# A fused two-layer trunk on one core: when the attention's queries and keys are prepared, and how close its steps stand together

## The chip, the core and the metric

The kernel is one program for one core of a Trainium2 chip. The core has a matrix engine (PE in the profile, with its weight loads shown apart as PEld), a vector engine (DVE), a scalar engine (ACT), a small general engine (POOL) and a queue that issues transfers (SP). Each works through its own list of instructions in a fixed order, and waits on semaphores for the others. The metric is the device time of one execution in microseconds (us), as the median of several runs.

## What is computed

A trunk of two layers over 512 positions of width 1024, all in float32. Layer 0 is forgetting attention with 16 heads of width 64, layer 1 a gated linear recurrence; each is followed by a gated feed-forward block with a causal convolution of width 3, and a last norm ends it. The change touches only the attention, which is in short:

```
proj = h @ w_in;  q, k, v, fl = split(proj)
c = cumsum(log_sigmoid(fl + b_f))                     # one running bias per head
logits = q @ k.T * scale + (c[t] - c[s])              # masked to s <= t
p = softmax(logits);  o = p @ v;  return o @ w_out
```

## The kernel before

**Precision and layout.** Activations are kept with the width on the 128 partitions and the 512 positions along the free axis. Each float32 matrix product is made of three products of a rounded high part and a low part (`mm3`, lines 85 to 87), so one 128x128 block of weights costs three matmuls over 512 columns. `chunk` loads a 512 KB block of weights into a `raw` tile (line 72) and `split` makes the high part on ACT (line 67) and the low part on DVE (line 68).

**Attention goes by pairs of heads.** Heads 2hp and 2hp+1 share 128 rows, so there are eight pairs. For a pair, `projections` makes three tiles of PSUM (values, queries, keys: `pj_v`, `pj_q`, `pj_k`, 24 matmuls each) and puts them in `queue`. It is the main stream of PE, and it runs up to three tiles ahead.

`operands` takes a tile from the queue. `values` scales and transposes it (`vT`) and splits it into `vh`, `vl`. `qk` scales it, splits it (ACT cast `qh` or `kh`, DVE subtraction `ql` or `kl`) and sends the pieces by small transfers into the four operand tiles `KX`, `QX`, `KK`, `QQ` of each head (lines 347 to 356). There are two sets of these tiles, so pair n writes over those of pair n-2.

`maxima` computes the row maxima of a pair: eight matmuls `mxp` (line 422) with `KX` and `QX`, each reduced on DVE (line 424, with a short read of the accumulator), in three PSUM banks named "s". The maxima go through a small transpose `rp` into `rrow` and by transfer into two more rows of `QX`.

`attend` does the softmax and the product with the values. `logits` makes one PSUM bank (`lg_a`, `lg_a`, `lg_c`, `lg_b`, `lg_b`, two banks in turn), takes the exponential on ACT into `pt` (line 464, two buffers), masks the diagonal blocks on POOL (line 466), casts on ACT to `ph` and subtracts on DVE to `pl`. `weigh` multiplies `ph` and `pl` with `vh`, `vl` into a bank `pv` (lines 480 to 482), `evacuate` copies it out on ACT (`dn`, `o`), and a reciprocal by logarithm and exponential on ACT (`rc`) with three DVE steps and a split gives `oh`, `ol`.

**What sets the order.** `conduct` (line 137) runs these generators together. Each turn takes one step of the main stream, which is one block of three matmuls, and then every side stream that is due. `yield 3` means due three turns later, `yield lambda: ...` means due as soon as the condition holds. Counters in `done` tie the streams together: `logits` counts pairs whose five logit tiles have been asked for, `out` counts pairs that are finished. A scheduler behind the language then lists the instructions of each engine, keeping near to the order in which they were asked for, but letting a later instruction pass an earlier one that it takes to be not ready. After the eighth pair the output projection `wo` takes over as the main stream (`early`), then the feed-forward block and the second layer, which the change does not touch.

Of the kernel before, what the change touches and what calls it, by code (L numbers as in the profile page):

```python
# [35 lines left out]
def trunk(ctx, tc, xT, gains, convs, bf, wqkv, wqkv0, wf, wo, wup, wdn, wh, wi, who, out):  # L36
# [12 lines left out]
    def side(name):  # L49

        return ps.tile([P, S], F32, tag="s", name=name)

    def lbank(name):
        return ps.tile([P, S], F32, tag="lg", name=name, bufs=2)
# [11 lines left out]
    def split(dst_h, dst_l, src):  # L66
        A.copy(dst_h, src)  # L67
        V.tensor_tensor(dst_l, src, dst_h.bitcast(F32), op=ALU.subtract)  # L68
# [161 lines left out]
    with tc.tile_pool(name="att", bufs=2, side="right") as ap_:  # L230
        def tmp(name, rows=P):
            return ap_.tile([rows, S], F32, tag="tmp", name=name, bufs=3)
# [13 lines left out]
        for i, (wa, wb, xa, xb) in enumerate(((0, 1, 0, 1), (1, 3, 1, 2), (3, 6, 2, 4), (6, 8, 4, 6), (8, 8, 6, 8))):  # L246
# [3 lines left out]
            if wb > wa:  # L250
                w = opool.tile([P, 4, 2, P], F32, name=f"wst{wa}", bufs=1, tag=f"ol{i}")
# [64 lines left out]
        def forget():  # L316

            z, e = tmp("fz", HEADS), tmp("fe", HEADS)
            A.copy(e, of[32:32 + HEADS])
            V.tensor_tensor(z, of[:HEADS], e, op=ALU.add)  # L320
            V.tensor_mul(z, z, rstd[:HEADS])
            V.tensor_scalar(z, z, bft, None, op0=ALU.add)
            V.scalar_tensor_tensor(e, z, -1.0, z, op0=ALU.mult, op1=ALU.max)
            A.activation(e, e, AF.Exp, scale=-1.0)
            A.activation(e, e, AF.Ln, bias=1.0)
            V.scalar_tensor_tensor(z, z, 0.0, e, op0=ALU.min, op1=ALU.subtract)
            m8 = tmp("m8", HEADS)
            G.memset(m8, 1.0)
            V.tensor_tensor_scan(e, m8, z, initial=0.0, op0=ALU.mult, op1=ALU.add)
            V.tensor_scalar(ch, e, -8.0, None, op0=ALU.mult)  # L330
            V.scalar_tensor_tensor(cl, e, -8.0, ch.bitcast(F32), op0=ALU.mult, op1=ALU.subtract)


        done = {"k": 0, "v": 0, "max": 0, "logits": 0, "out": 0}

        def qk(w, hp, o):
            nm = "qk"[w]
            t32 = tmp(f"{nm}32_{hp}")
            V.tensor_mul(t32, o, rstd)
            th = ap_.tile([P, S], F32R, tag="pth", name=f"{nm}h_{hp}", bufs=1)  # L340
            tl = ap_.tile([P, S], F32R, tag="ptl", name=f"{nm}l_{hp}", bufs=1)
            split(th, tl, t32)
            th, tl = th.bitcast(F32), tl.bitcast(F32)
            for e in range(2):
                r = slice(64 * e, 64 * e + 64)
                t = {n: a.bitcast(F32) for n, a in st[2 * (hp % 2) + e].items()}
                if w == 0:
                    nc.sync.dma_start(t["QX"][0:64], th[r])
                    nc.sync.dma_start(t["QQ"][0:64], tl[r])
                    nc.sync.dma_start(t["QQ"][64:128], th[r])  # L350
                else:
                    h = 2 * hp + e
                    nc.sync.dma_start(t["KX"][64:66], cc[h:h + 33:32].bitcast(F32))
                    nc.sync.dma_start(t["KX"][0:64], th[r])
                    nc.sync.dma_start(t["KK"][0:64], th[r])
                    nc.sync.dma_start(t["KK"][64:128], tl[r])
            done["k"] += w
# [18 lines left out]
        queue = []  # L376
# [16 lines left out]
        def operands():  # L393

            forget()
            qk(0, 0, oq)
            qk(1, 0, ok)
            values(0, ov)
            for hp in range(8):
                for w, n in ((2, hp), (0, hp + 1), (1, hp + 1)):  # L400
                    if n == 8 or (hp == 0 and w == 2):
                        continue
                    yield lambda: queue and done["out"] >= n - 1
                    w_, n_, o = queue.pop(0)
                    if w == 2:
                        values(n, o)
                    else:
                        qk(w, n, o)
# [33 lines left out]
        def attend():  # L442

            for hp in range(8):
                yield lambda: done["max"] > hp and done["v"] > hp
                yield 5
                tt = [st[2 * (hp % 2)], st[2 * (hp % 2) + 1]]
                vh, vl = vst[hp % 2]
                parts = {}

                def logits(key, *blocks):

                    nm = f"{hp}_{key}"
                    lg = lbank(f"lg_{nm}")
                    w = 0
                    for e, j, c in blocks:
                        n = S - P * j
                        reg = lg[:, c:c + n]
                        js = slice(j * P, (j + 1) * P)
                        t = tt[e]  # L460
                        PE.matmul(reg, t["KK"][:, js], t["QQ"][:, j * P:], start=True, stop=False)
                        PE.matmul(reg, t["KX"][0:68, js], t["QX"][0:68, j * P:], start=False, stop=True)
                    pt = ap_.tile([P, S], F32, tag="pt", name=f"pt_{nm}", bufs=2)
                    A.activation(pt, lg, AF.Exp, scale=0.125)
                    for e, j, c in blocks:
                        G.affine_select(out=pt[:, c:c + P], in_=pt[:, c:c + P], pattern=[[1, P]],
                                        compare_op=ALU.is_ge, fill=0.0, base=0, channel_multiplier=-1)
                    ph = ap_.tile([P, S], F32R, tag="ph", name=f"ph_{nm}", bufs=3)
                    pl = ap_.tile([P, S], F32R, tag="pl", name=f"pl_{nm}", bufs=3)
                    split(ph, pl, pt)  # L470
                    for e, j, c in blocks:
                        parts[e, j] = ph, pl, c

                def weigh(o, e, js):
                    cs = slice(64 * e, 64 * e + P)
                    for j in js:
                        ph, pl, c = parts[e, j]
                        s_ = slice(c, c + S - P * j)
                        oo = o[:, j * P:]
                        PE.matmul(oo, vh[:, j, cs], ph[:, s_], start=j == 0, stop=False)  # L480
                        PE.matmul(oo, vl[:, j, cs], ph[:, s_], start=False, stop=False)
                        PE.matmul(oo, vh[:, j, cs], pl[:, s_], start=False, stop=j == 2)

                dn = ap_.tile([P, S], F32, tag="dn", name=f"dn_{hp}", bufs=1)
                o32 = ap_.tile([P, S], F32, tag="o32", name=f"o32_{hp}", bufs=1)

                def evacuate(o, e):
                    a, b = slice(64 * e, 64 * e + 64), slice(64 - 64 * e, 128 - 64 * e)
                    A.copy(dn[a], o[b])
                    A.copy(o32[a], o[a])  # L490

                logits("a0", (0, 0, 0))
                yield 3
                logits("a1", (0, 1, 0), (0, 3, 384))
                yield 3
                logits("c", (0, 2, 0), (1, 2, 256))
                yield 3
                oa = side(f"pv_{hp}_0")
                weigh(oa, 0, (0,))
                logits("b0", (1, 0, 0))  # L500
                yield 2
                weigh(oa, 0, (1, 3))
                logits("b1", (1, 1, 0), (1, 3, 384))
                done["logits"] += 1
                yield 3
                weigh(oa, 0, (2,))
                evacuate(oa, 0)
                ob = side(f"pv_{hp}_1")
                weigh(ob, 1, (0,))
                yield 2  # L510
                weigh(ob, 1, (1, 3, 2))
                evacuate(ob, 1)
                rc = tmp(f"rc_{hp}")
                A.activation(rc, dn, AF.Ln)
                A.activation(rc, rc, AF.Exp, scale=-1.0)
                V.tensor_mul(dn, dn, rc)
                V.scalar_tensor_tensor(rc, dn, 2.0, rc, op0=ALU.subtract, op1=ALU.mult, reverse0=True)
                V.tensor_mul(o32, o32, rc)
                if hp % 2 == 0:
                    pair[:] = [opool.tile([P, 2, S], F32R, tag=f"{n}{hp // 2}", name=f"{n}{hp}", bufs=1)  # L520
                               for n in ("oh", "ol")]
                oh[hp], ol[hp] = (t[:, hp % 2] for t in pair)
                split(oh[hp], ol[hp], o32)
                done["out"] += 1
# [62 lines left out]
    with tc.tile_pool(name="hg", bufs=2, side="right") as hp_:  # L587
# [46 lines left out]
        done = {"core": 0, "out": 0}  # L634
# [270 lines left out]
```

## Time and profile before

| | |
|---|---|
| median of 3 runs | 1275.78 us (1275.57 to 1275.93) |
| the profiled execution, its own time | 1276.34 us |
| its span, from first to last instruction | 1274.6 us |
| PE busy | 1254.7 us, 98% of the span |
| DVE, ACT, POOL busy | 803.9, 590.8, 45.7 us |
| chain that ended last, share of PE | 93% |
| the attention's pairs, by the trace | about 50 to 240 us after the start |

A matmul that is issued right behind another starts about 0.23 us after it when it has 512 columns, though the profile shows it as 0.39 us long: matmuls overlap in the array. So time lost on PE is best read from the distance between starts. The idle time in brackets behind a row is shorter than that.

### The profile page before, as it was taken

The numbers are of one execution on the slowest core, as the hardware profiler recorded it, in microseconds if no ns is written. First come the engines' busy times: TensorE is split into PE (matmuls) and PEld (weight loads), VectorE is DVE, ScalarE is ACT, GpSimd is POOL, SyncE is SP. The second block draws the span as 40 slices with busy tenths as digits, with TensorE's granted clock in tenths as the row PEclk, the third lists the DMA queues.
The fourth block names the chain that finished last, engine by engine and source line by source line (L and its number), as shares of the span: only waits on it lengthen the run. The fifth ranks groups of instructions, "written<-read, shape, count | busy, mean of one in ns | idle before, by whom it ended". The sixth has DMA issues, their size and how long they took to land.

```text
span 1274.6 us, 15662 instructions
## 1 busy us (share of the span) xinstructions
PE 1254.7 (98%) x6002; PEld 1041.3 (82%) x6002; DVE 803.9 (63%) x1230; ACT 590.8 (46%) x830; POOL 45.7 (4%) x121
## 2 busy tenths in 40 slices
PE   8999999999999999999999999999999999999996
PEld 6777888888888888888888988987888888888886
DVE  6687667387777777333367585566777777762233
ACT  6366556464444444222266565554544444442231
POOL 2011110000000000000010000000000000000001
PEclk9999999999999999999999999999999999999999
DMA  5643454243333233333322222223233333323321
GB/s 179 170 135 98 130 130 132 83 133 99 100 100 99 93 93 93 91 96 102 95 84 83 81 69 83 84 67 91 91 100 99 100 98 91 94 89 94 97 83 66
DMA packets 42586, 127.25 MB, mean 100 GB/s; under 512 B 5536, under 2 KB 7840, under 8 KB 42512
## 3 DMA queue, kind: packets, MB, share of 16 engines
q1 hardware_dynamic: 41728, 125.52, 33.1%
q8 instruction: 47, 0.77, 0.3%
q10 hardware_dynamic: 688, 0.56, 0.1%
q0 software_dynamic: 96, 0.18, 0.1%
q14 instruction: 27, 0.22, 0.1%
HBM read 111.43 MB, written 2.10 MB: 89 GB/s over the span
## 4 chain that ended last, share of the span: by engine, by line
PE 93%; DVE 2%; ACT 2%; DMA 1%; issue 1%; POOL 0%; SPq 0%; DVEq 0%; ACTq 0%
PE pj_up L87 13%; PE pj_up L85 13%; PE pj_up L86 13%; PE pj_dn L85 6%; PE pj_dn L87 6%; PE pj_dn L86 6%; PE i L651 1%; PE i L650 1%; PE i L648 1%; PE pj_who L86 1%; PE pj_wo L85 1%; PE pj_wo L86 1%; PE pj_who L87 1%; PE pj_who L85 1%; PE pj_wo L87 1%; PE pj_hf L85 1%
## 5 line engine op out<-in xcount | busy, mean ns | idle before, releaser
L85 PE MATMUL pj_up<-xh_f,wh_up 128*128 128x512 f32 x704 | 273.9, 389 | 0.0
L86 PE MATMUL pj_up<-xl_f,wh_up 128*128 128x512 f32 x704 | 273.9, 389 | 0.0
L87 PE MATMUL pj_up<-xh_f,wl_up 128*128 128x512 f32 x704 | 273.9, 389 | 0.0
L86 PEld LDWEIGHTS pj_up<-xl_f,wh_up 128*128 128x128 f32 x704 | 132.1, 188 | 27.6
L87 PEld LDWEIGHTS pj_up<-xh_f,wl_up 128*128 128x128 f32 x704 | 132.1, 188 | 27.4
L85 PEld LDWEIGHTS pj_up<-xh_f,wh_up 128*128 128x128 f32 x704 | 132.1, 188 | 27.3
L85 PE MATMUL pj_dn<-gh,wh_dn 128*128 128x512 f32 x330 | 130.8, 396 | 0.0
L86 PE MATMUL pj_dn<-gl,wh_dn 128*128 128x512 f32 x330 | 130.8, 396 | 0.0
L87 PE MATMUL pj_dn<-gh,wl_dn 128*128 128x512 f32 x330 | 130.8, 396 | 0.0
L67 ACT CAST wh_up<-raw_up 128x1024 fp32r<-128x1024 f32 x88 | 92.7, 1053 | 65.8 <-PE pj_up L86 50.7
L68 DVE TENSOR_TENSOR wl_up<-raw_up,wh_up 128x1024 fp32r<-128x1024 f32 x88 | 107.8, 1225 | 15.3 <-ACT wh_up L67 11.7
L68 DVE TENSOR_TENSOR wl_dn<-raw_dn,wh_dn 128x1024 fp32r<-128x1024 f32 (+1 forms) x45 | 51.1, 1136 | 98.2 <-ACT wh_dn L67 98.0
L560 DVE TENSOR_TENSOR us<-pj_up,rstd_f 128x512 f32<-128x512 f32 x88 | 60.6, 688 | 78.4 <-PE pj_up L87 78.2
L67 ACT CAST wh_dn<-raw_dn 128x1024 fp32r<-128x1024 f32 (+1 forms) x45 | 44.1, 980 | 140.4 <-PE pj_dn L86 109.1
L67 ACT CAST gh<-y 128x512 fp32r<-128x512 f32 x44 | 27.3, 620 | 115.5 <-DVE y L568 115.5
L563 ACT ACTIVATE y<-us,cv 128x512 f32<-128x512 f32 x88 | 71.7, 815 | 8.5 <-DVE us L560 7.3
L87 PEld LDWEIGHTS pj_dn<-gh,wl_dn 128*128 128x128 f32 x330 | 62.2, 188 | 15.2
L86 PEld LDWEIGHTS pj_dn<-gl,wh_dn 128*128 128x128 f32 x330 | 62.2, 188 | 15.2
L85 PEld LDWEIGHTS pj_dn<-gh,wh_dn 128*128 128x128 f32 x330 | 62.1, 188 | 15.1
L565 DVE SCALAR_TENSOR_TENSOR y<-us,cv,y 128x512 f32<-128x512 f32 x88 | 66.2, 752 | 3.0
L564 DVE SCALAR_TENSOR_TENSOR y<-us,cv,y 128x512 f32<-128x512 f32 x88 | 65.6, 746 | 0.2
L567 ACT ACTIVATE y<-y 128x512 f32<-128x512 f32 x44 | 27.8, 632 | 79.5 <-DVE y L565 79.5
(372 smaller groups left out, 2383.6 us busy)
## 6 DMA issues: line engine op xcount, KB each, us to landing
raw_up<-in_wup SPq DMA_DIRECT2D x88, 512.0 KB
raw_dn<-in_wdn SPq DMA_DIRECT2D x30, 512.0 KB
raw_dn<-in_wdn SPq DMA_DIRECT2D x15, 384.0 KB
raw_v<-in_wqkv SPq DMA_DIRECT2D x8, 512.0 KB
raw_wo<-in_wo SPq DMA_DIRECT2D x8, 512.0 KB
raw_hf<-in_wh SPq DMA_DIRECT2D x8, 512.0 KB
raw_hq<-in_wh SPq DMA_DIRECT2D x8, 512.0 KB
raw_hg<-in_wh SPq DMA_DIRECT2D x8, 512.0 KB
```

The lines of the kernel that those rows point to most:

```text
L67: A.copy(dst_h, src)
L68: V.tensor_tensor(dst_l, src, dst_h.bitcast(F32), op=ALU.subtract)
L85: PE.matmul(o, wh_, xh_, start=first, stop=False)
L86: PE.matmul(o, wh_, xl_, start=False, stop=False)
L87: PE.matmul(o, wl_, xh_, start=False, stop=last)
L560: V.tensor_mul(u[:, 2:], o, rstd)
L563: A.activation(y, u[:, 2:], AF.Identity, scale=k(2), bias=k(3))
L564: V.scalar_tensor_tensor(y, u[:, 1:S + 1], k(1), y, op0=ALU.mult, op1=ALU.add)
L565: V.scalar_tensor_tensor(y, u[:, 0:S], k(0), y, op0=ALU.mult, op1=ALU.add)
L567: A.activation(ys[0], ys[0], AF.Silu)
L648: PE.matmul(o, xh[kk][:, ts_], hs, start=kk == 0 and i % 2 == 0, stop=False, skip_group_check=True)
L650: PE.matmul(o, xh[kk][:, ts_], ls, start=False, stop=False, skip_group_check=True)
```

## The change

In `operands`, queries and keys of pair n no longer wait until pair n-2 is finished (`done["out"]`), only until its five logit tiles have been asked for (`done["logits"]`). Values wait as before. In `attend`, six waits become two turns long: the one ahead of a pair (five before) and four of those between its steps (three before). The other two stay at two. Together the steps of one pair are asked for over 12 turns instead of 21. No instruction is added or taken away.

```diff
@@ operands
-                    yield lambda: queue and done["out"] >= n - 1
+
+                    yield lambda: queue and done["out" if w == 2 else "logits"] >= n - 1
@@ attend
                 yield lambda: done["max"] > hp and done["v"] > hp
-                yield 5
+                yield 2
...
                 logits("a0", (0, 0, 0))
-                yield 3
+                yield 2
                 logits("a1", (0, 1, 0), (0, 3, 384))
-                yield 3
+                yield 2
                 logits("c", (0, 2, 0), (1, 2, 256))
-                yield 3
+                yield 2
                 oa = side(f"pv_{hp}_0")
...
                 done["logits"] += 1
-                yield 3
+                yield 2
                 weigh(oa, 0, (2,))
```

The engines' lists show it at three places. Names carry buffer numbers; lines move by one. The pairs are counted from 0.

PE, the steps of one pair. Before, pair 4, from the end of its last logit tile `lg_b` to the product of tile c with the values; nine projection matmuls stand between, of which the list shows all:

```order
L462 MATMUL lg_b_1650<-QX_316,KX_315 128x128
L85 MATMUL pj_v_1620<-xh_a_132,wh_v_0_1623 128x512
L86 MATMUL pj_v_1620<-xl_a_133,wh_v_0_1623 128x512
L87 MATMUL pj_v_1620<-xh_a_132,wl_v_0_1624 128x512
L85 MATMUL pj_v_1620<-xh_a_146,wh_v_0_1623 128x512
L86 MATMUL pj_v_1620<-xl_a_147,wh_v_0_1623 128x512
L87 MATMUL pj_v_1620<-xh_a_146,wl_v_0_1624 128x512
L85 MATMUL pj_v_1620<-xh_a_161,wh_v_0_1623 128x512
L86 MATMUL pj_v_1620<-xl_a_162,wh_v_0_1623 128x512
L87 MATMUL pj_v_1620<-xh_a_161,wl_v_0_1624 128x512
L480 MATMUL pv_0_1603<-ph_c,vh_338 128x256
```

The same place now, in pair 3:

```order
L463 MATMUL lg_b_1347<-QX_328,KX_327 128x128
L481 MATMUL pv_0_1321<-ph_c,vh_342 128x256
L482 MATMUL pv_0_1321<-ph_c,vl_343 128x256
L483 MATMUL pv_0_1321<-pl_c,vh_342 128x256
L481 MATMUL pv_1_1371<-ph_b_1331,vh_342 128x512
L482 MATMUL pv_1_1371<-ph_b_1331,vl_343 128x512
L483 MATMUL pv_1_1371<-pl_b_1332,vh_342 128x512
L86 MATMUL pj_q_1485<-xl_a_133,wh_q_0_1488 128x512
```

The projection matmuls have moved out from between the steps. From the first matmul of a pair with the finished `QX` to its last `weigh`, pair 3 now has eight of them between its steps (two behind `lg_a`, one, four, one), and before, pair 4 had 48. They stand in one run behind the pair instead.

ACT, the end of a pair and the cast `kh` of the next pair's keys. Before (end of pair 3, `kh` for pair 4):

```order
L464 ACTIVATE pt_b_1346<-lg_b_1343 128x512
L67 CAST wh_v_0_1623<-raw_v_0_1621 128x1024
L67 CAST ph_b_1349<-pt_b_1346 128x512
L67 CAST kh_1368<-k_4_1366 128x512
L464 ACTIVATE pt_b_1391<-lg_b_1386 128x512
L67 CAST ph_b_1395<-pt_b_1391 128x512
```

Now, the same cast:

```order
L491 COPY o_3_1247<-pv_0_1321 64x512
L490 COPY dn_1246<-pv_1_1371 64x512
L491 COPY o_3_1247<-pv_1_1371 64x512
L515 ACTIVATE rc_1392<-dn_1246 128x512
L516 ACTIVATE rc_1392<-rc_1392 128x512
L67 CAST kh_1415<-k_4_1413 128x512
```

The cast of the next pair's keys has moved from between two tiles of the pair to behind its copies and its reciprocal.

DVE, what stands ahead of the first reduction of the row maxima (`mxp`) of pair 4. Before:

```order
L68 TENSOR_TENSOR pl_b_1350<-pt_b_1346,ph_b_1349 128x512
L68 TENSOR_TENSOR kl_1369<-k_4_1366,kh_1368 128x512
L68 TENSOR_TENSOR pl_b_1396<-pt_b_1391,ph_b_1395 128x512
L424 ISA mxp_0_0_1421,mx_1420<-mxp_0_0_1421,maskw 128x128
L424 ISA mx_1420 128x1
```

Now:

```order
L517 TENSOR_TENSOR dn_1246<-dn_1246,rc_1392 128x512
L68 TENSOR_TENSOR kl_1416<-k_4_1413,kh_1415 128x512
L518 SCALAR_TENSOR_TENSOR rc_1392<-dn_1246,rc_1392 128x512
L339 TENSOR_TENSOR q_5_1573<-pj_q_1485,rstd_a 128x512
L519 TENSOR_TENSOR o_3_1247<-o_3_1247,rc_1392 128x512
L68 TENSOR_TENSOR wl_k_0_1833<-raw_k_0_1830,wh_k_0_1832 128x1024
L68 TENSOR_TENSOR ol_1133<-o_3_1247,oh_1132 128x512
L425 ISA mxp_0_0_1440,mx_1439<-mxp_0_0_1440,maskw 128x128
```

The finishing of the pair, which stood behind the next pair's maxima, now stands ahead of them.

## Rows read from the trace of the kernel before

**Rows 1.** The page: the span, and the chain that ended last by engine.

```profile
span 1274.6 us, 15662 instructions
PE 93%; DVE 2%; ACT 2%; DMA 1%; issue 1%; POOL 0%; SPq 0%; DVEq 0%; ACTq 0%
```

**Rows 2.** Stretches: start:end, length, busy time of PE, PEld, DVE, ACT, POOL, clock, DMA.

```profile
60.00:126.00 66.00, 61.84 (x312) 48.82 (x311) 49.35 (x107) 40.13 (x66) 10.83 (x24) 1.00 0.46 124
126.00:228.00 102.00, 101.15 (x506) 83.20 (x506) 72.98 (x150) 58.48 (x95) 11.79 (x33) 1.00 0.49 130
```

**Rows 3.** Waits of PE from 42 to 250 us: total, times, longest.

```profile
PE lg_c L461 <- ACT pt_a L464: 1.1, 2, 0.5
PE mxp L422 <- DMA KX<-kh: 1.0, 1, 1.0
...
PE mxp L422 <- DVE mx L424: 0.6, 3, 0.2
...
PE pv L480 <- ACT vh L370: 0.2, 1, 0.2
```

**Rows 4.** Timeline of PE in pair 1: start, length, what, [idle before, releaser].

```profile
76.38 0.39 PE L87 MATMUL pj_v<-xh_a,wl_v 128*128 128x512 f32 x1
77.29 0.39 PE L461 MATMUL lg_c<-QQ,KK 128*128 128x256 f32 x1 [0.52 <-ACT pt_a L464]
77.52 0.28 PE L462 MATMUL lg_c<-QX,KX 68*128 68x256 f32 x1
77.64 0.28 PE L461 MATMUL lg_c<-QQ,KK 128*128 128x256 f32 x1
```

**Rows 5.** Timeline of PE in pair 0, the first logit tiles.

```profile
60.63 0.57 PE L462 MATMUL lg_a<-QX,KX 68*128 68x512 f32 x2
...
61.21 0.45 PE L87 MATMUL pj_k<-xh_a,wl_k 128*128 128x512 f32 x1
61.71 0.39 PE L461 MATMUL lg_c<-QQ,KK 128*128 128x256 f32 x1
```

**Rows 6.** Timeline of ACT in pair 0: exponentials, casts, and a cast of weights.

```profile
61.06 1.09 ACT L464 ACTIVATE pt_a<-lg_a 128x512 f32<-128x512 f32 x2 [1.59 <-PE lg_a L462]
62.05 1.35 ACT L67 CAST ph_a<-pt_a 128x512 fp32r<-128x512 f32 x2
63.30 1.05 ACT L67 CAST wh_k<-raw_k 128x1024 fp32r<-128x1024 f32 x1
```

**Rows 7.** Timeline of POOL, two selects of a tile: in pair 0 and in pair 2.

```profile
62.21 0.54 POOL L466 TENSOR_SCALAR_AFFINE_SELECT pt_a<-pt_a 128x128 f32<-128x128 f32 x2 [0.19 <-ACT pt_a L464]
107.79 1.75 POOL L466 TENSOR_SCALAR_AFFINE_SELECT pt_b<-pt_b 128x128 f32<-128x128 f32 x2 [0.17 <-ACT pt_b L464]
```

**Rows 8.** Timeline of DVE: two steps in a row in pair 1, weights in pair 2.

```profile
78.40 0.68 DVE L68 TENSOR_TENSOR ql<-q,qh 128x512 fp32r<-128x512 f32 x1
79.00 0.69 DVE L517 SCALAR_TENSOR_TENSOR rc<-dn,rc 128x512 f32<-128x512 f32 x1
107.39 1.31 DVE L68 TENSOR_TENSOR wl_v<-raw_v,wh_v 128x1024 fp32r<-128x1024 f32 x1
```

**Rows 9.** Timeline of ACT and PE at the end of pair 2.

```profile
111.31 0.62 ACT L67 CAST kh<-k 128x512 fp32r<-128x512 f32 x1
114.45 0.63 ACT L515 ACTIVATE rc<-rc 128x512 f32<-128x512 f32 x1
...
112.27 0.28 PE L482 MATMUL pv<-pl_c,vh 128*128 128x256 f32 x1
114.23 0.50 PE L422 MATMUL mxp<-KX,QX 66*128 66x128 f32 x2 [0.99 <-DMA KX<-kh]
```

**Rows 10.** Timeline of DVE and PE: reductions of the row maxima, and a wait for one.

```profile
114.60 0.30 DVE L424 CUSTOM_DVE_ANT_0 mxp<-mxp,maskw 128x128 f32<-128x128 f32 x1 [1.94 <-PE mxp L422]
...
114.82 0.47 DVE L424 CUSTOM_DVE_ANT_0 mxp<-mxp,maskw 128x256 f32<-128x256 f32 x1
...
140.58 0.50 PE L422 MATMUL mxp<-KX,QX 66*128 66x512 f32 x1 [0.22 <-DVE mx L424]
```

## The prediction

> **What bounds the kernel now.** I read the page first, for the bound: the chain that ended last is 93% PE [rows 1], so a change pays only where it moves PE's start times. The edits leave PE's own work alone. What they can give or take is PE's waiting in the attention, and I read that next by stretches: PE is idle 4.16 us of the 66 us of pairs 0 to 2, and 0.85 us of the 102 us behind them, at a granted clock of 1.00 in both (2.4 GHz) [rows 2]. Then the waits of PE, for who is waited for: eight lines, twelve waits, nearly all of them for a step of the softmax (exponential, cast, subtraction), three for a reduction of the maxima, one for a transfer of keys [rows 3].
>
> Idle time is less than what a wait costs. In the timeline the next matmul after a projection matmul should start 0.23 later; with 0.52 shown as idle it started 0.91 later, so it was 0.68 late, 0.16 more than shown, and the step behind it took 0.23 instead of 0.12, another 0.1 [rows 4]. So I count each wait as its idle time plus 0.26. A wait may also show next to no idle time and still make a matmul late: 61.21 to 61.71 is 0.50 where 0.23 is the rule [rows 5]. Of such small ones I counted some eight, and put them at 2 us.
>
> PE's late starts now are then 5.0 idle + 12 x 0.26 + 2 = **10.2 us**: about 7.7 in pairs 0 to 2 and 2.5 in the rest. That is all that the change can win back, and pairs 3 to 7 have almost nothing to give.
>
> **The change, part by part.** *What is asked for earlier.* By the lists the wait on the logits wins nothing by itself: since a pair now also ends sooner, the cast of the next keys stands behind the pair's copies and reciprocal on ACT, not between its tiles. It is later against its pair, not earlier.
>
> *The steps of a pair stand close together.* Before, 48 projection matmuls (48 x 0.23 = 11 us) lay between the steps of pair 4 and hid every tile's way through ACT, POOL, ACT, DVE. Now eight do. I follow one pair, with time 0 at the first `lg_a` matmul on the finished `QX`. The steps: exponential 0.43 after that matmul's start, 0.60 long, the next 0.49 behind it [rows 5, 6]; select 0.54 for two blocks, some 0.06 after its exponential, half of that for one block [rows 7]; cast 0.62, the next 0.5 behind [rows 6]; subtraction 0.69, the next 0.60 behind [rows 8]; 0.05 for each hop from engine to engine (exponentials done at 62.15, select at 62.21 [rows 6, 7]).
>
> Pairs 1, 3, 5, 7 have the cast of a weight tile just ahead of the first exponential. It may start when a projection ends, at about -0.3, and holds ACT 0.95 [rows 6], so the exponential runs 0.65 to 1.25. PE has done `lg_a` and two projection matmuls at 1.04 and waits for it until 1.30: late 0.26 + 0.10. The first cast is done at 2.26 and PE comes for it at 2.35: nothing. Second tile: exponential to 1.74, select to 2.34, cast to 3.01, subtraction to 3.75; PE wants it at 3.62, late 0.18. Tile c: exponential to 3.5 (behind the casts), select to 4.09, cast to 4.76; PE comes at 4.77, late 0.04, has 0.24 to do with the cast part, and then needs the subtraction, done at 5.50: late 0.50. Fourth tile: late 0.05. Fifth: its logits end at 4.77, exponential to 5.78, select to 6.37, cast (behind a copy) to 7.2; PE has four projection matmuls and comes at 7.28: nothing for the cast, 0.13 for the subtraction. Sum **1.25 us**.
>
> Pairs 0, 2, 4, 6 have that weight cast in the middle and one projection matmul less behind `lg_a`. By the same steps: 0.37 at `lg_c`; 0.32 for the cast of tile c (1.05 of weights ahead of it [rows 6]); 0.27 for its subtraction; 0.30 for the fourth cast, whose exponential now stands behind; 0.23 for the last subtraction: **1.5 us**. What neither sum has is a select that is slowed: two blocks took 0.54 where DVE was quiet and 1.75 where it ran a weight subtraction of 1.31 [rows 7, 8]. If that meets tile c or the last one, it adds 0.5 to 0.6 each. I take 1.5 for every pair, and 1.2 to 2.5 as bounds.
>
> *The maxima of the next pair.* Keys first. From the last `weigh` matmul, ACT's reciprocal exponential starts 2.18 later [rows 9]; the key cast follows 0.53 behind and ends at 3.34. A key cast that ended at 111.93 let `mxp` start at 114.23 [rows 9], 2.30 later, so `mxp` may start at 5.64. PE has 24 projection matmuls first, 24 x 0.23 = 5.5: late 0.1 to 0.2. On SP the transfer stands behind a small one and a weight load that ask for nothing late; its issue costs nothing more. Second, the finishing of the pair now stands ahead of the reductions on DVE: seven steps from 2.86 on, six of 0.60 and one of 1.2 [rows 8], so the first reduction starts at 7.7 and frees its bank at 8.0 (0.30 long [rows 10]). PE has filled all three banks at 6.1, does six projection matmuls and two logit matmuls, and wants the fourth at 7.9: late 0.15 + 0.1; the next waits for the second reduction (0.47 long, 0.22 behind [rows 10]), late 0.16. Together with the keys **0.6 us**. Now a pair's maxima wait too, 0.22 idle for one of them [rows 10]; those late starts are in the 10.2.
>
> *Values, outputs and the end.* Values keep their wait. At the end the output projection still has some 37 matmuls (8.4 us) behind the last `weigh` before it needs the last pair; finishing takes 2.18 + 0.63 on ACT [rows 9], five steps on DVE [rows 8] and a cast, under 7 us. Nothing is late there.
>
> *Sum.* After: 8 x 1.5 + 7 x 0.6 = 16.2 us of late starts. Before: 10.2. Difference **+6.0 us**. Pairs 0 to 2 come out about 1.5 better (7.7 against three times 2.1), since their stretch loses the mix with the pair before; pairs 3 to 7 about 7.5 worse. The profiled execution took 1276.34, with 1.74 outside its span, so it would become 1282.3; the median of the runs lies 0.56 lower, which gives **1281.8**.
>
> **Rivals.** A measurement of this kernel can tell about 0.2% from no change, 2.55 us, so with 4.2 for the maxima what decides is a pair's price in its bunch: under 0.44 us is faster, 0.44 to 1.06 the same, above it slower.
>
> *The bunch costs next to nothing, and the kernel is faster.* Between the bunches ACT and DVE now run almost free, and a tile that is early by a few tenths removes most of my late starts, which are 0.1 to 0.5 each. With 0.2 per pair: 8 x 0.2 + 4.2 = 5.8, 4.4 less than now: 1271.4. For it: pair 0 of the trace has its tiles close together too and shows 0.05 of idle at `lg_c` [rows 5]. Against it: the subtraction of tile c is 0.69 and PE has 0.24 to do meanwhile, whatever comes before. Chance 0.12.
>
> *Pairs 0 to 2 win what the others lose.* At 0.8 per pair: 8 x 0.8 + 4.2 = 10.6, +0.4: 1276.2. For it: 7.7 of the 10.2 lies in pairs 0 to 2. Against it: it needs the sums above wrong by half. Chance 0.20.
>
> *POOL is blocked in every bunch.* With the subtractions of five tiles now within some 5 us, a select meets one of them more often; twice per pair at 0.5 makes 2.5 per pair: 8 x 2.5 + 4.2 = 24.2, +14: 1289.8. For it: 1.75 against 0.54 [rows 7]. Against it: in my chain only one select in a pair overlaps a subtraction for long, and the next step often has slack. Chance 0.17. The Trainium skill (SBUF — State Buffer, Who interferes with whom) speaks for this one: a VectorE instruction with two SBUF inputs and a GpSimd instruction that reads SBUF exclude each other, and the second to issue blocks until the first is done. The long selects agree with it, and by it the time would lie at this rival's.
>
> **How the numbers follow.** The forecast, late starts of 1.06 to 2.1 per pair, 0.51; it is the likeliest, so 1281.8. Slower by over 0.2%: 0.51 + 0.17 = 0.68; within 0.2%: 0.20; faster: 0.12. The range leaves out most of the faster case and half of the blocked one: 1272.5 to 1288.
>
> **What would show it.** Right: PE idle behind 126 us rises from 0.85 to 4 us or more, with waits for `ph_c`, `pl_c` and `pt_a` once in every pair; `mxp` waits for DVE or `KX` in each pair; PE's idle time in pairs 0 to 2 falls below 4.16; nothing moves behind the attention but by the shift. Wrong: PE busy to 9 tenths without such waits in pairs 3 to 7, or selects of 1 us and more on POOL in each pair, or a wait of 1 us for `KX` or `QX` in each pair.

## The result, and the profile after

The changed kernel takes **1287.93 us** (median of 4 runs, 1286.54 to 1288.51) beside 1275.86 for the kernel before: a ratio of 1.0086, 95% interval 1.0073 to 1.0099. It is slower by some 12 us. The forecast was 1281.8, slower, with a range of 1272.5 to 1288.0: the sign is right, the time lies at the very end of the range, and half of the loss was not foreseen. Two of the four executions lie above 1288.0, so it is luck that the median falls inside the range, by 0.07.

The profiled execution took 1288.51. Its page has the span and the chain of [rows 1] as

```profile
span 1286.8 us, 15686 instructions
...
PE 83%; issue 6%; DVE 4%; ACT 3%; DMA 2%; POOL 1%; SPq 0%; DVEq 0%; ACTq 0%; POOLq 0%
```

PE's share of the chain fell from 93% to 83%. The stretches of [rows 2], and one more for the pairs that now end later (start:end, length, busy time of PE, PEld, DVE, ACT, POOL, granted clock, DMA share, GB/s):

```profile
60.00:126.00 66.00, 62.21 (x288) 47.92 (x287) 42.20 (x85) 39.51 (x64) 8.08 (x24) 0.95 0.40 114
126.00:228.00 102.00, 99.02 (x476) 76.59 (x474) 66.28 (x143) 55.26 (x88) 11.26 (x32) 1.00 0.44 121
228.00:262.00 34.00, 32.90 (x159) 26.37 (x160) 17.42 (x38) 15.33 (x27) 2.21 (x8) 1.00 0.20 55
```

Behind 126 us PE's idle time went from 0.85 to 2.98 + 1.10 = 4.08 us. Between 60 and 126 us it is a little less than before (3.79 against 4.16), and yet PE got through 288 matmuls there, not 312. Part of that is the clock, which was granted at 0.95 in that row, and part are late starts without idle time. The waits of PE from 42 to 262 us (total, times, longest):

```profile
PE pv L481 <- ACT ph_c L67: 1.5, 2, 1.0
PE pj_v L85 <- DVE v L362: 1.4, 1, 1.4
PE pv L481 <- ACT ph_b L67: 1.2, 2, 0.8
PE pv L483 <- DVE pl_c L68: 1.1, 5, 0.2
PE pv L481 <- ACT ph_a L67: 1.1, 3, 0.4
PE mxp L423 <- DVE mx L425: 0.2, 1, 0.2
```

(The change adds a line of code, so L480 of the kernel before is L481 here.) The keys' wait of [rows 3] is gone, `pl_c` is waited for in five pairs, and one line is new in kind: a projection matmul that waits 1.40 us for DVE.

Idle time leaves out what [rows 4] showed, late starts without idle time. So I also took, for each step of PE, the distance to the next start less the usual distance for steps of that line and shape (0.227 for a projection matmul), and summed this excess by stretch. Before and after, in us:

| stretch, us | 0–43.5 | 43.5–60 | 60–100 | 100–126 | 126–256 | 256–300 | 300 to the end |
|---|---|---|---|---|---|---|---|
| before | 7.55 | 0.42 | 6.26 | 3.81 | 8.23 | 0.53 | 14.9 |
| after | 6.60 | 0.39 | 10.94 | 3.03 | 15.84 | 1.48 | 15.0 |
| difference | -0.95 | 0 | +4.68 | -0.78 | **+7.61** | +0.95 | +0.1 |

The sum is 11.6 of the 12.15 us between the spans. With another choice of the usual distance the entries change, but the differences stay at 4.7 to 5.8 from 60 to 100 us, -0.7 to -1.3 up to 126 us and 7.5 to 8.2 behind it. The first column is not the change's: the profiled execution of the kernel before has a stretch at a granted clock of 0.5 from 9.92 to 13.33 us, that of the kernel after has none there. Of the kernels below some have it and some don't. Two places remain: the pairs from 126 us on, and the stretch from 60 to 100 us.

**A pair's bunch.** PE in pair 4 (start, length, operation):

```profile
164.58 0.45 PE L87 MATMUL pj_v<-xh_a,wl_v 128*128 128x512 f32 x1
165.08 0.39 PE L462 MATMUL lg_c<-QQ,KK 128*128 128x256 f32 x1
165.31 0.28 PE L463 MATMUL lg_c<-QX,KX 68*128 68x256 f32 x1
165.43 0.28 PE L462 MATMUL lg_c<-QQ,KK 128*128 128x256 f32 x1
...
168.58 0.28 PE L463 MATMUL lg_b<-QX,KX 68*128 68x128 f32 x1
168.96 0.38 PE L481 MATMUL pv<-ph_c,vh 128*128 128x256 f32 x1
169.19 0.28 PE L482 MATMUL pv<-ph_c,vl 128*128 128x256 f32 x1
169.30 0.39 PE L87 MATMUL pj_v<-xh_a,wl_v 128*128 128x512 f32 x1
169.69 0.39 PE L483 MATMUL pv<-pl_c,vh 128*128 128x256 f32 x1
169.92 0.40 PE L85 MATMUL pj_q<-xh_a,wh_q 128*128 128x512 f32 x1
```

164.58 to 165.08 is 0.50 where 0.23 is the rule: 0.27 late for the bank that the first exponential frees. The cast of tile c makes 168.96 late by 0.21, its subtraction 169.69 by 0.16; four more such places make 1.42 us for the pair. Summed in the same way (starts late by over 0.1 us), pairs 1 to 7 cost 1.37, 1.32, 1.39, 1.42, 1.38, 2.16 and 1.26. This sum leaves out most of the 0.1 that the step behind each late one loses as well (165.31 comes 0.23 behind 165.08, not 0.12). With these small ones the pairs cost some 1.7 to 2.1 each, and pair 6 some 2.65.

**The stretch at 60 us.** In pair 0, DVE, POOL, ACT and PE:

```profile
63.47 1.23 DVE L68 TENSOR_TENSOR wl_k<-raw_k,wh_k 128x1024 fp32r<-128x1024 f32 x1 [0.26 <-ACT wh_k L67]
...
63.99 1.10 POOL L467 TENSOR_SCALAR_AFFINE_SELECT pt_c<-pt_c 128x128 f32<-128x128 f32 x2 [2.17 <-ACT pt_c L465]
...
65.12 0.62 ACT L67 CAST ph_c<-pt_c 128x512 fp32r<-128x512 f32 x1 [0.71 <-POOL pt_c L467]
...
65.80 0.39 PE L481 MATMUL pv<-ph_c,vh 128*128 128x256 f32 x1 [1.02 <-ACT ph_c L67]
```

The select that takes 0.54 when DVE is quiet [rows 7] took 1.10 beside a weight subtraction, and PE waited 1.02 for the cast behind it. Seven microseconds later:

```profile
72.36 0.70 DVE L425 CUSTOM_DVE_ANT_0 mxp<-mxp,maskw 128x512 f32<-128x512 f32 x1
...
72.97 0.69 DVE L362 TENSOR_TENSOR v<-pj_v,rstd_a 128x512 f32<-128x512 f32 x1
...
73.72 0.80 PE L85 MATMUL pj_v<-xh_a,wh_v 128*128 128x512 f32 x1 [1.40 <-DVE v L362]
...
74.31 0.63 PE L86 MATMUL pj_v<-xl_a,wh_v 128*128 128x512 f32 x1
...
74.74 0.63 PE L87 MATMUL pj_v<-xh_a,wl_v 128*128 128x512 f32 x1
...
75.16 0.63 PE L85 MATMUL pj_v<-xh_a,wh_v 128*128 128x512 f32 x1
```

All projection banks are full, and the step that frees one, DVE's scaling of the values, stands in DVE's list behind the eight reductions of pair 1's maxima. Then the projection matmuls start 0.43 apart, not 0.23, and take 0.63, not 0.39. The granted clock of that stretch, 72.85 to 79.67 us, is 0.5 (the lower level, 1.2 GHz), where the kernel before has 1.00:

```profile
72.85:79.67 6.83, 5.96 (x19) 4.78 (x20) 6.47 (x13) 3.69 (x6) 0.00 (x0) 0.50 0.26 60
```

PE's 5.96 busy us there would be about half as long at the upper level: some 3 us are lost to the clock, an estimate from this row and the two distances. The mean granted clock is 0.995 or 0.996 in all four executions, and 0.997 in the profiled one of the kernel before, so the profiled one is probably not alone in this loss.

### The profile page after: what moved, and what is told of

It reads as the page before. It is cut to its first block, busy times and chain, and to the rows that moved or that the text cites. A ratio compares the mean times of both kernels' runs of the same rounds, so it can differ in the third digit from the quotient of the medians.

```text
span 1286.8 us, 15686 instructions
## 1 busy us (share of the span) xinstructions
PE 1262.9 (98%) x6002; PEld 1040.2 (81%) x6002; DVE 800.4 (62%) x1230; ACT 592.8 (46%) x830; POOL 42.9 (3%) x121
## 4 chain that ended last, share of the span: by engine, by line
PE 83%; issue 6%; DVE 4%; ACT 3%; DMA 2%; POOL 1%; SPq 0%; DVEq 0%; ACTq 0%; POOLq 0%
PE pj_up L87 12%; PE pj_up L86 12%; PE pj_up L85 12%; PE pj_dn L85 6%; PE pj_dn L87 6%; PE pj_dn L86 6%; PE i L652 1%; PE i L651 1%; PE i L649 1%; PE pj_who L86 1%; PE pj_who L87 1%; PE pj_who L85 1%; PE pj_hf L85 1%; PE pj_hf L86 1%; PE pj_hf L87 1%
## 5 line engine op out<-in xcount | busy, mean ns | idle before, releaser
L68 DVE TENSOR_TENSOR wl_up<-raw_up,wh_up 128x1024 fp32r<-128x1024 f32 x88 | 107.8, 1225 | 15.1 <-ACT wh_up L67 11.6
```

## The experiments

The theories. **A**: two causes; every bunched pair costs 1.4 us because too few matmuls lie between its tiles, and the stretch at 60 us costs 4.5 us of its own. **B**: the price is the same for each pair and nothing else counts. **C**: POOL's selects, held by DVE, are what costs. **D**: where a pair starts counts, not how close its steps stand. The letters below say which is meant, and later texts add theories of their own.

One part of the change needed no run. With the old distances the new condition on the queue leaves the list of every engine as it was, row by row; with the new distances the old condition gives the lists of the kernel after. The condition by itself is without effect in this change.

**1. Pair 0 as before, the rest as after.**

```diff
-                yield 2
+                yield 5 if hp == 0 else 2
...
-                yield 2
+                yield 3 if hp == 0 else 2
```

(and so for the other distances)

> The kernel after, but pair 0 asks for its steps at the old distances (5, then 3, 3, 3, 2, 3, 2); pairs 1 to 7 stand bunched as in the kernel after. Theory A (two causes: some 1.4 us of late starts in every bunched pair, and some 4.5 us in the stretch from 60 to 80 us alone, where PE waits 1.40 for a projection bank and then runs at a granted clock of 0.5): the stretch goes back to what it was before, the bank wait and the half clock are gone, and 4 to 5 us of the 12 come back: 1282.5 to 1284. Theory B (the price is the same in every pair, and the stretch at 60 us is nothing of its own): an eighth of 12 comes back, 1286.4. Theory C (POOL's select blocked by DVE is what costs, in every bunch): 1286 to 1287, with selects above 1 us in most of the pairs 1 to 7.

Measured: 1283.35 (1.0063, 1.0050 to 1.0076). 4.6 us came back, as theory A said. PE's waits in the profile have neither the 1.0 for `ph_c` nor the 1.4 for a bank, the longest is 0.6, and the clock stays at 1.00 from 60 to 280 us. This profile is of the shortest of the five executions (1280.89, with a mean granted clock of 0.998; the other four have 0.995 to 0.997), so what the clock did in the others is not shown. Theory B, 1286.4, and theory C, 1286 to 1287, are out.

**2. Pair 0 alone bunched.** The same edit the other way round, in the kernel before.

> The kernel before, but pair 0 alone asks for its steps two apart; pairs 2 to 7 stand as before. Theory A: the wait for a select in pair 0 (1 us) returns, and if the bank wait and the half clock come with it, 1279.5 to 1281; pairs 3 to 7 show next to no idle time, as before. If the half clock needs the maxima of pair 1 in one heap behind the bunch, which this kernel doesn't have, only 1 to 1.5 us: 1277 to 1277.5. Theory B: an eighth of 12, 1277.4. Theory C: 1277.4.

Measured: 1278.79 (1.0022, 1.0014 to 1.0031), +2.95. That is a miss for every theory: A put it 0.7 higher at least, B and C 1.4 lower. The waits of PE from 42 to 100 us, and the first stretch:

```profile
PE pj_v L85 <- DVE v L362: 1.4, 1, 1.4
PE pv L480 <- ACT ph_c L67: 1.4, 2, 1.0
```

```profile
60.00:126.00 66.00, 62.06 (x301) 48.90 (x300) 47.92 (x106) 39.13 (x65) 8.60 (x25) 0.97 0.44 124
```

Both waits are back, and with them a stretch at 0.5, from 74.19 to 77.61 us, half as long as in the kernel after. The excess from 60 to 100 us is 10.3, +4.0 against before; pair 2 behind it gives 1.6 back, and that is why the total is below the forecast. Between 126 and 256 us it is 8.3, as before. So pair 0's bunch by itself brings on most of that stretch (+4.0 of the +4.68), and changes nothing behind 126 us. Ten of the eleven executions have a mean granted clock of 0.994 or 0.995 and took 1278.1 to 1280.2; the eleventh, at 0.997, took 1276.51. No trace of that one is kept, but it hints that most of the 2.95 is the clock's.

**3 and 4. The first distance alone (5 to 2), and the inner distances alone (3 to 2).** By the diff the change shortens five waits, not six: the first, and four of the six inner ones. A pair's steps are asked for over 14 turns in place of 21; without the first wait it is 12 in place of 16.

```diff
-                yield 5
+                yield 2
```

> The kernel before with one number changed: the first step of a pair waits for 2 projection steps in place of 5; the five inner distances stay 3, 3, 3, 2, 3, 2. In the lists pairs 2 and 3 become bunched as in the kernel after, in pairs 4 to 7 six to nine projection matmuls still stand between the weighing of one tile and the next, only the first four logits stand together. Theory A: pairs 2 and 3 cost 1.4 each, pairs 4 to 7 0.4 to 0.8 each for the first tile, no bank wait at 72 us: 1278 to 1281. Theory C: selects collide only in the bunched pairs: 1277 to 1279. Theory D (where the pair starts, not how close its steps stand, is what costs): all of the 12, 1287.

```diff
                 logits("a0", (0, 0, 0))
-                yield 3
+                yield 2
```

(and so for the three others)

> The kernel before with the inner distances alone changed: 2, 2, 2, 2, 2, 2 behind a first step that still waits for 5. In the lists the pairs 3 to 7 have five to six projection matmuls between the tiles that were nine apart before, and two to five between the reductions of the maxima. Theory A: the cover of 5 to 6 matmuls (1.2 to 1.4 us) is enough for most tiles, so pairs 3 to 7 cost 0.3 to 0.6 each and pairs 0 and 1 about 2 together: 1277 to 1280. Theory C: 1280 to 1283, with selects above 1 us in most pairs. Theory D: as the kernel before, within 1 us of 1275.9.

The first distance alone: 1278.32 (1.0021, 1.0012 to 1.0029), within A's bounds and C's. Theory D, 1287, is out for these distances. The excess from 152 to 230 us, where the lists again have six to nine matmuls between tiles, is 5.3; before it was 5.0. The inner distances alone: 1284.71 (1.0068, 1.0056 to 1.0080), a miss for all three theories. From 126 to 262 us the only wait above the small ones is

```profile
PE mxp L422 <- DMA KX<-kh: 5.3, 4, 1.6
```

The tiles, with five to six matmuls between them, cost 0.27 a pair there, at `lg_c`, and no more, so the cover does what A says. But now the keys of the next pair come late to its maxima, and behind the longest of these waits stands another stretch at 0.5, from 172.71 to 176.13. A theory of tiles alone can't price such an edit: the distances also shift the pairs against the work on the queue.

One wait of this run bears on the stretch at 60 us. PE waits 1.40 here too for DVE's scaling of pair 1's values, and the granted clock stays at 1.00 (the wait, and the stretch around it):

```profile
76.69 0.66 PE L366 MATMUL vT<-ident,v 128*128 128x128 f32 x4 [1.40 <-DVE v L362]
```

```profile
60.00:126.00 66.00, 61.32 (x295) 46.92 (x294) 46.32 (x103) 38.90 (x64) 9.29 (x24) 1.00 0.43 117
```

So such a wait doesn't always bring the half clock with it.

**5. The values scaled ahead of pair 1's maxima** (the kernel after).

```diff
                 yield lambda: done["k"] > hp
-                yield 4
+                yield 8 if hp == 1 else 4
```

> The kernel after with one number changed: the maxima of pair 1 wait for 8 projection steps in place of 4. In DVE's list the scaling of the values of pair 1 (which frees the projection bank that PE waited 1.40 for at 71.8 us) now stands ahead of the eight reductions of that pair, not behind them; pair 0 is still bunched, and its wait of 1 us for a select may stay. Theory A1 (the bank wait brings the half clock about): both go, and 4 to 4.5 us of the 12 come back: 1283.4 to 1284. Theory A2 (the half clock follows from the wait for the select, or from the bunch itself): only the bank wait goes, and an interval at 0.5 stays in the records between 65 and 85 us: 1286 to 1287. Theory B (that wait is hidden behind something else): 1287 to 1288.5.

Measured: 1291.64 (1.0120, 1.0107 to 1.0133), worse than after, and outside of what any theory gave. The bank wait is gone and so is the stretch at 0.5 behind it; the excess from 60 to 100 us fell from 10.9 to 8.4, for two new waits of 0.8 and 0.9 took the place. The lists of the later pairs shifted too: waits for keys of 1.18 and 1.27, a pair 6 with waits of 1.02 and 0.85, and two stretches at 0.5, from 211.05 and 231.53 us. The wait of 1.01 for the select in pair 0 stayed, and no stretch at 0.5 followed it, against theory A2. That the clock fell because of the bank wait is consistent with this, but the run doesn't isolate it, and run 4 has a wait as long without it.

**6. Short selects** (the kernel after; the mask is left out on 120 of each block's 128 columns).

```diff
-    G.affine_select(out=pt[:, c:c + P], in_=pt[:, c:c + P], pattern=[[1, P]],
+    G.affine_select(out=pt[:, c:c + 8], in_=pt[:, c:c + 8], pattern=[[1, 8]],
```

> The kernel after with POOL's select cut to 8 of its 128 columns in every tile (the causal mask on a tile's diagonal block is left out for the other 120); the order on every engine is the same as in the kernel after. A tile's way to PE becomes some 0.4 us shorter, and no select can be held for long by DVE. Theory A (the price of a bunch is the length of a tile's way through ACT, POOL, ACT and DVE): a pair falls from 1.4 us of late starts to 0.5 to 0.8, the wait for the select in pair 0 and what follows it shrink too: 1278 to 1282. Theory C (blocked selects are what costs): only pairs 0 and 6 gain, where the trace shows selects of 1.10 and 1.54 on the path, 1 us each and perhaps the half clock: 1283 to 1286, and pairs 2 to 5 stay at 1.3 to 1.4 each. Theory E (exponentials and subtractions set the price, selects lie beside them): no change in pairs 1 to 5, 1286 to 1288.

Measured: 1283.22 (1.0058, 1.0046 to 1.0070), 4.7 less than the kernel after. The time is just inside C's bounds and above A's; the pairs fit neither. A quiet select fell from 0.54 to 0.33, but the long ones stayed long (DVE and POOL in pair 0):

```profile
63.84 1.23 DVE L68 TENSOR_TENSOR wl_k<-raw_k,wh_k 128x1024 fp32r<-128x1024 f32 x1 [0.20 <-ACT wh_k L67]
...
64.37 0.89 POOL L467 TENSOR_SCALAR_AFFINE_SELECT pt_c<-pt_c 128x8 f32<-128x8 f32 x2 [2.17 <-ACT pt_c L465]
```

Sixteen columns took 0.89 and ended at 65.26, 0.19 behind the end of DVE's step at 65.07. So the select is held until DVE's subtraction is done, however short its own work is. The Trainium skill (SBUF — State Buffer, Who interferes with whom) says that a VectorE step with two SBUF inputs and a GpSimd step that reads SBUF exclude each other, so that the second waits until the first is done; these two rows agree. My expectation that no short select could be held was wrong, and the run separates A from C less well than meant. What it does show, pair by pair: in pairs 2 to 5 the price went from 1.32–1.42 to 1.07–1.23, 0.15 to 0.25 each (0.2 to 0.5 with the small late starts behind), since most late starts there wait for an exponential or a subtraction; pair 6, where no select was held any longer, went from 2.16 to 0.98. Its row in the kernel after:

```profile
225.99 1.54 POOL L467 TENSOR_SCALAR_AFFINE_SELECT pt_b<-pt_b 128x128 f32<-128x128 f32 x2 [2.44 <-ACT pt_b L465]
...
228.24 0.44 PE L481 MATMUL pv<-ph_b,vh 128*128 128x384 f32 x1 [0.77 <-ACT ph_b L67]
```

Theory C is then true of pair 6, 1.2 us, and by its held select (1.10 for 0.54) of some 0.6 us in pair 0, but not of the rest. Part of the 4.7 is the clock: the stretch at 0.5 is 3.41 us long here, from 74.13 us, where the kernel after has 6.83.

**7 and 8. The other direction: inner distances 4, 4, 4, 3, 4, 3** with the new condition, with the old first distance of 5 and with 2.

```diff
                 logits("a0", (0, 0, 0))
-                yield 3
+                yield 4
```

> The other direction: the new condition on the queue, the old first distance of 5, and inner distances of 4, 4, 4, 3, 4, 3. In the lists nine to twelve projection matmuls stand between the tiles of pairs 2 to 7. Theory A (late starts come where a tile has too little cover): pairs 3 to 7 had 2.5 us of late starts in all and keep 1 to 2.5 of them, pairs 0 to 2 gain what the cover gives, up to 3: 1272.5 to 1276. Theory F (the work that the pairs no longer hide moves somewhere else: a wait for keys, for the maxima, or at the output projection): 1277 to 1281, with a new wait of 1 us or more.

> As the wider kernel (the new condition, inner distances of 4, 4, 4, 3, 4, 3), but with the new first distance of 2. Theory A: as the wider kernel, 1272.5 to 1277, since six to twelve projection matmuls stand between the tiles. Theory D (where a pair starts is what costs): 1280 or more. Theory F: 1277 to 1281, with a new wait of 1 us or more for keys or maxima.

Measured: 1280.81 (1.0048, 1.0034 to 1.0063) and 1290.37 (1.0111, 1.0098 to 1.0124). In the first, the excess from 60 to 204 us is 10.0 where the kernel before has 15.7: nine to twelve matmuls of cover win some 5 us in the pairs where they stand. All of it and more is lost at the end, as theory F says. PE's waits from 204 to 272 us:

```profile
PE pj_wo L85 <- ACT oh L67: 3.7, 2, 2.6
PE lg_c L461 <- ACT pt_a L464: 1.6, 1, 1.6
```

The last pairs come so late that the output projection has nothing left to do but wait for them. The second is far above the bounds of A and F; only theory D's "1280 or more" holds it. So where a pair starts does count once the pairs are wide, 9.6 us between these two runs, by the way of the keys: in the second, keys are late to the maxima (7.0 us in four waits, 3.09 the longest), and the output projection waits 1.9 besides. PE behind that longest wait, at a granted clock of 0.5 from 114.59 to 121.41 us:

```profile
114.67 1.12 PE L422 MATMUL mxp<-KX,QX 66*128 66x128 f32 x3 [3.09 <-DMA KX<-kh]
...
116.44 0.63 PE L85 MATMUL pj_q<-xh_a,wh_q 128*128 128x512 f32 x1
116.86 0.63 PE L86 MATMUL pj_q<-xl_a,wh_q 128*128 128x512 f32 x1
```

**9 to 11. Wide pairs first, old distances at the end.** Four wide pairs, five, and four with the old condition on the queue.

```diff
-                yield 3
+                yield 4 if hp < 4 else 3
```

> The wider kernel for pairs 0 to 3 (new condition on the queue, inner distances 4, 4, 4, 3, 4, 3), the old inner distances 3, 3, 3, 2, 3, 2 for pairs 4 to 7. In the lists nine projection matmuls stand between the tiles of pairs 4 to 7, and six matmuls stand inside the last pair, as before, with the output projection behind it. Theory A (the cover of each tile sets the price, and what the wider kernel lost it lost at the end, where its last pair came too late for the output projection): it keeps the some 5 us that the wider kernel won between 60 and 204 us, and the waits of 2.6 and 0.84 behind 250 us are gone: 1269.5 to 1273. Theory F (wider pairs move work to the end whatever the last pairs do): 1276 to 1281 with waits of 1 us or more behind 200 us.

> As the kernel with four wide pairs, but five (pairs 0 to 4). In the lists the logits of the last pair come somewhat closer together (nine, three, none, none, nine projection matmuls between the tiles). Theory A: within 2 us of the one with four wide pairs, 1269.5 to 1274. Theory F: 1276 to 1281.

> As the kernel with four wide pairs, but with the old condition on the queue (queries and keys wait for the finished pair two back). With narrow pairs the two conditions give the same lists; here they don't: in the lists each pair now weighs its tiles in one heap, behind the maxima of the next. Theory A (cover alone counts, tiles are long done when the heap comes): 1269.5 to 1274. Theory G (the condition matters here, since the keys of the next pair come later against its maxima): 1276 to 1283, with waits of 1 us or more for keys, queries or maxima in pairs 2 to 6.

Measured: 1274.33 (0.9991, 0.9982 to 1.0000), 1274.48 (0.9991, 0.9982 to 1.0000) and 1281.54 (1.0048, 1.0034 to 1.0061). The first two miss A's bounds by 1.3 and 0.5, and stay below F's. The win between 60 and 204 us stays in the first (10.8 against 15.7). The end was underrated: the output projection still waits 1.21 for the finished pair and then 0.70 for an addition on DVE that empties a bank, 2.2 us with what follows. The third lies within theory G's bounds: the maxima wait 6.3 us for keys, in four waits of up to 2.50: the condition that does nothing between narrow pairs is worth 7 us between wide ones.

**12. As 9, with pair 7 asked for early** (a first distance of 2, then 2 each).

```diff
-                yield 4 if hp < 4 else 3
+                yield (4, 4, 4, 4, 3, 3, 3, 2)[hp]
```

(and so for the others; the first distance is 2 for pair 7)

> As the kernel with four wide pairs, but pair 7 asks for its steps two apart with a first distance of 2, so that it ends 18 projection matmuls (4.1 us) sooner against the output projection; in its list six matmuls stand between its tiles. Theory A: the waits for the finished pair in the output projection (1.21 and 0.70 idle, 2.24 late) go, the last pair's tiles are still covered by six matmuls: 1271.5 to 1273, 2 us less than with four wide pairs. Theory H (these waits move elsewhere, or the closer last pair costs as much as it gives): 1274 to 1276, as with four wide pairs or no better than the kernel before.

Measured: **1271.47** (1270.97 to 1272.65; 0.9965, 0.9951 to 0.9978), faster than both kernels and at the lower bound of theory A. PE's waits from 42 to 272 us, and the stretches:

```profile
PE mxp L422 <- DVE mx L424: 1.4, 4, 0.6
PE mxp L422 <- DMA KX<-kh: 1.1, 1, 1.1
PE lg_c L461 <- ACT pt_a L464: 0.5, 1, 0.5
```

```profile
60.00:126.00 66.00, 64.96 (x330) 52.83 (x330) 47.45 (x105) 41.76 (x67) 11.10 (x24) 1.00 0.53 142
126.00:228.00 102.00, 99.71 (x506) 82.79 (x505) 70.18 (x151) 59.25 (x96) 13.44 (x35) 1.00 0.44 120
228.00:262.00 34.00, 34.00 (x156) 27.93 (x155) 19.92 (x29) 19.48 (x31) 1.54 (x6) 1.00 0.29 94
```

330 matmuls in the first stretch, where [rows 2] has 312 and the kernel after 288, and no idle time from 228 to 262 us. POOL is busy for as long here as before the change (11.10 and 13.44 us in the first two rows, 10.83 and 11.79 in [rows 2]), and in pair 1 a select is held for longer than in either kernel:

```profile
88.86 2.03 POOL L466 TENSOR_SCALAR_AFFINE_SELECT pt_b<-pt_b 128x128 f32<-128x128 f32 x2 [3.90 <-ACT pt_b L464]
```

No matmul of that tile starts late by over 0.1 us. In these runs a held select costs only where the tile behind it has no cover.

## Why the prediction was half right, step by step

- *What PE waits for now.* Loosely read: of the twelve waits in [rows 3] six, not nearly all, are for a step of the softmax; and 5.0 + 12 x 0.26 + 2 is 10.1, not 10.2. Neither moves the forecast by more than 0.1.
- *A bunch costs 1.5 us per pair.* **Right in mechanism, a little small**: 1.26 to 1.42 in six of the seven pairs from 1 on, but the forecast counts the step behind each late one too, and so counted they cost 1.7 to 2.1, within its bounds of 1.2 to 2.5. The first steps were met one by one: in pair 4 `lg_c` was put at 0.37 late, the cast of c at 0.32 and its subtraction at 0.27, and they measured 0.27, 0.21 and 0.16, each with 0.1 behind it. In the odd pairs a late start of 0.5 for `ph_a` was not in the chain (the weight cast ahead of the exponential also puts the select beside DVE's weight subtraction), and the 0.18 for `pl_a` didn't come.
- *Pairs 3 to 7 about 7.5 us worse.* Right: +7.61 from 126 to 256 us. Misses cancel in it: the pairs cost more, pair 6 above all, the maxima less. That the sum is met so closely is luck.
- *The maxima, 0.6 us per pair.* **Over-sized**: 0.13 to 0.33. No matmul of the kernel after waits for keys, and one waits for a reduction with idle time, 0.2. The sign that `mxp` would wait in each pair did not come.
- *Pairs 0 to 2 about 1.5 us better.* **This step failed.** It took pair 0 for a pair like the others and the clock for constant. From 60 to 126 us the excess rose by 3.9. Three things follow on one another there: a select held by 0.56 (1.10 for 0.54), in the tile that had no slack (the working named this case and its 0.5, as a bound); the values' scaling behind the heap of reductions, so that a *projection* bank comes late by 1.40, where the working had looked at the banks of the maxima alone; and 6.83 us at half the clock. Runs 1 and 2 show that they come and go with pair 0's bunch.
- *The condition wins nothing.* Right, and stronger than put: it changes no list.
- *Nothing late behind the attention.* Nearly right: +0.95 to 300 us, nothing behind.
- *The rival of the blocked POOL, 1289.8.* Its time is nearest to the result, and yet its mechanism isn't the cause: held selects stand in seven of eight pairs, but cost much in two of them alone, some 0.6 us in pair 0 and 1.2 us in pair 6. The mark that was to prove the forecast wrong, selects of 1 us in each pair, was badly chosen: it looked at POOL, not at who waits.

By stretches: 6.0 forecast, plus 0.1 for the pairs 3 to 7, plus 5.4 for the pairs 0 to 2 (+3.9 in place of -1.5), plus 0.95 behind 256 us, less the 0.95 ahead of 43.5 us that isn't the change's, gives 11.5 of the 12.15 us between the two spans. What stays open is how much of pair 0's stretch is the bank wait and how much the clock, and why the clock fell: run 4 has a wait as long at 1.00, but at other distances, and no run changed the one alone.

## What to carry to other kernels

Where a filler stream (here the projections) hides a chain through several engines, count the filler between a chain's steps, not their total: eight matmuls between five tiles cost 1.4 us a pair and more, five to six between each two 0.27 (run 4), nine next to nothing, and a held engine was then free too. The filler is a budget: cover given to early pairs was missing for the last, so of the orders tried here the best was wide first and narrow at the end. And when steps are moved together, look at every buffer that the moved heap stands in front of, not only at the heap's own.

## What the runs showed of the hardware

- **The clock fell near short waits of a busy PE.** Behind 43 us and up to 300 us, the thirteen other traces have ten stretches at 0.5, of 3.41 or 6.83 us. Each began within an idle time of PE, or within 2 us behind one, of 0.85 to 3.09 us; the kernel before has one of 0.99 there [rows 9] and no such stretch. The reverse doesn't hold: 32 idle times were over 1 us, most were not followed by one, not even the 2.6 in run 7. In the kernel after, the wait of 1.40 and the 6.83 us at 0.5 that began in it cost some 4 us together (an estimate from the 1.40 and the some 3 us above).
- **A held select waits for the end of DVE's step, not for a share of it**: eight columns for each of two blocks took 0.33 by themselves and 0.89 beside a weight subtraction, ending 0.19 behind it.
